# Up projection: six row tiles in halves, operands one tile ahead, another order of banks; final norm of the first half among the last products

## The chip, the cores and the metric

One core of one Trainium2 chip runs the whole program in one launch. The metric is the device time of one execution in microseconds (us); the median of three runs is quoted. TensorE (PE) multiplies, VectorE (DVE) and ScalarE (ACT) prepare operands and evacuate results, GpSimd (POOL) issues some DMAs, SyncE (SP) issues most of them.

## The reference, cut to what matters

A diffusion block over 512 latent tokens of width 2048: attention and a short convolution with adaLN modulation, an output projection with a gated residual, and then the part that is changed:

```
hf_l = modulate(rms_norm(x, g_ffn_norm), sh_f, sc_f)
u = dwconv3(hf_l @ w_up, cw, cb)          # 2048 -> 2 x 5504, width-3 convolution over tokens
a, g = jnp.split(u, 2, axis=-1)
x = x + gt_f * ((a * silu(g)) @ w_down)   # 5504 -> 2048
return rms_norm(x, g_final)
```

All of it is float32. Each float32 product is made of three products of rounded parts (high by high, high by low, low by high).

## The kernel before

**Layout.** Activations lie transposed: 16 tiles of 128 features by 512 tokens. An operand is a pair of tiles, `h` (rounded by ACT, a CAST) and `l` (the rest, a subtraction on DVE). `mm3` issues the three products; L168, L169 and L170 are its lines.

**First pairs of the up projection.** The 86 column tiles of `w_up` go in 43 pairs (gate and value). The first three pairs (`G` = 6 column tiles, tiles `uf`) are made row by row: for each of the 16 row tiles k, `first_weights(k)` loads and splits 6 weight tiles (`ufr`, `ufw`), `hf_tile(k)` normalises and modulates x (times `rl` on DVE at L854, scale and shift on ACT at L855, CAST at L857, subtraction at L858), and `row` issues 18 products. The first `EARLY` = 4 row tiles are made in token halves `H0` and `H1`, since the norm of `H0` is known before that of `H1`; their weights are held for both. `t_sums(j)` forms sums of halves (`T`, and new values in the second halves of `hf`) for the other 40 pairs, which a scheme with seven smaller products per pair makes (`product`, tiles `u3` to `u42`).

**Norms.** `rms_steps` is a generator: products with ones over the squares (L281), square root on ACT (L259), reciprocal on DVE (L260), a product that spreads the result over partitions (L265), a copy to `rl` (L288). `pump` takes it a step further between other work.

**Banks.** PSUM has eight banks. As built, `uf` has banks 7, 4, 5, 6 (pair 0's gate and value, pair 1's) and 2 and 3 (pair 2's). `bank8` then hands out banks in turn, three per pair (a, b, c), so u3 has banks 0, 1 and 2. `acts` frees the banks of `uf` pair by pair (convolution at L921 to L923, Silu at L929).

**The end.** The last group of the down projection has four output tiles (12 to 15); its last 8 of 43 row tiles are made for `H0`, then for `H1`. Per output tile and half that is 24 products, `down_end` (residual, DVE at L1127) and the square (ACT). The final norm of `H0` runs amid the products of `H1`; `final` multiplies by it (DVE at L1134) and stores two tiles at a time, eight stores of 256 KB per half, all from SP (L1135).

**What sets the order.** The program is written in the order of the source, but a scheduler of the tile framework orders each engine's instructions when it builds. Engines then run their own lists in order and wait for one another by semaphores.

Of the kernel before, what the change touches and what calls it, by code (L numbers as in the profile page):

```python
# [10 lines left out]
F32 = mybir.dt.float32  # L11
F32R = mybir.dt.float32r
AF = mybir.ActivationFunctionType
ALU = mybir.AluOpType
# [3 lines left out]
P = 128  # L18
# [3 lines left out]
NK = D // P  # L22
# [8 lines left out]
ORDER = [*range(7, 25), *range(7), *range(25, 31)]  # L31
G = 6

EARLY = 4

BANKS = [0, 1, 7, 4, 5, 6, 2, 3]
CTX_EARLY = 6
# [3 lines left out]
LAST = 8  # L41

AHEAD = 3


_SM = {}
# [12 lines left out]
def block_kernel(ctx, tc, xt, ctxt, ctxn, c, c_ctx, w_ada, small, w_in, w_inc, w_q, w_kv, w_out,  # L59
# [115 lines left out]
    def pump(n=1):  # L175
        while n and bg:
            if next(bg[0], bg) is bg:
                bg.popleft()
            else:
                n -= 1  # L180

    def drain():
        pump(-1)
# [14 lines left out]
    rl = con.tile([P, T], F32, name="rl")  # L198
# [617 lines left out]
    def row(pss, w, x, k, cols=slice(0, T)):  # L816

        for g in range(G):
            mm3(pss[g][:, cols], w[g], tuple(z[:, cols] for z in x), k == 0 and cols.start == 0, k == NK - 1)
# [25 lines left out]

    hf = {}

    def hf_tile(j, cols=slice(0, T)):
        if j not in hf:
            hf[j] = tuple(t2([P, T], F32R, f"hf{j}{z}") for z in "hl")  # L850
        sc = tiny(1, f"fs{j}")
        scale_of(sc, s("g_ffn", j), mod[:, 64 + j:65 + j])
        xr = xres[j][:, cols]
        V.tensor_tensor(out=xr, in0=xr, in1=rl[:, cols], op=ALU.mult)  # L854
        A.activation(xr, xr, AF.Identity, bias=mod[:, 48 + j:49 + j], scale=sc)  # L855
        hi, lo = (z[:, cols] for z in hf[j])
        A.copy(out=hi, in_=xr)  # L857
        V.tensor_tensor(out=lo, in0=xr, in1=hi.bitcast(F32), op=ALU.subtract)  # L858

    def hf_early():  # L860
        for j in range(3):
# [64 lines left out]
    def acts(f, g, a):  # L926

        ug = conv3(NF + f, g, f"g{f}")
        A.activation(ug, ug, AF.Silu)  # L929
        ua = conv3(f, a, f"a{f}")  # L930
        V.tensor_tensor(out=ua, in0=ua, in1=ug, op=ALU.mult)  # L931
        G_.dma_start(y_d[f], ua)  # L932
# [11 lines left out]
    def t_sums(j):  # L944

        e, o = xres[2 * j], xres[2 * j + 1]
        i, c = j // 2, HS[j % 2]
        if j % 2 == 0:
            for n in (1, 2, 4):
                TT[n, i] = tuple(t2([P, T], F32R, f"T{n}{i}{z}") for z in "hl")  # L950

        def put(dst, src):
            hi, lo = dst
            A.copy(out=hi, in_=src)
            V.tensor_tensor(out=lo, in0=src, in1=hi.bitcast(F32), op=ALU.subtract)

        V.tensor_tensor(out=e[:, H0], in0=e[:, H0], in1=e[:, H1], op=ALU.subtract)
        V.tensor_tensor(out=e[:, H1], in0=o[:, H1], in1=e[:, H1], op=ALU.subtract)
        put(half_of(hf[2 * j], 1), e[:, H1])
        V.scalar_tensor_tensor(out=o[:, H1], in0=e[:, H0], scalar=-1.0, in1=o[:, H1], op0=ALU.mult, op1=ALU.subtract)  # L960
        V.scalar_tensor_tensor(out=o[:, H0], in0=o[:, H1], scalar=-1.0, in1=o[:, H0], op0=ALU.mult, op1=ALU.subtract)
        for n, src in ((1, e[:, H0]), (2, o[:, H1]), (4, o[:, H0])):
            put(tuple(z[:, c] for z in TT[n, i]), src)
# [8 lines left out]
    def first_weights(k, held=False):  # L972

        raw = raw4(f"ufr{k}")
        SP.dma_start(raw[:, :G * P], w_up_first[k // 2][:, k % 2 * G * P:(k % 2 + 1) * G * P])
        if held:
            w = [hilo(raw[:, a:a + n], n, f"ufw{k}_{a}") for a, n in ((0, 4 * P), (4 * P, 2 * P))]
            return [part(w[g // 4], g % 4) for g in range(G)]
        w = split4(raw[:, :G * P], G * P, f"ufw{k}")
        return [part(w, g) for g in range(G)]  # L980
# [10 lines left out]
        return r  # L991

    pss = first_banks("uf")
    held = {}
    for h in range(2):
        for k in range(EARLY):
            if h == 0:
                held[k] = first_weights(k, k == EARLY - 1)
            if h or k > 2:
                hf_tile(k, HS[h])  # L1000
            row(pss, held[k], hf[k], k, HS[h])
            pump(1)
            if h and k % 2:
                t_sums(k // 2)
        drain()
    for k in range(EARLY, NK):
        if k == NK - 4:
            raws = up_load(G // 2)
        w = first_weights(k)
        hf_tile(k)  # L1010
        row(pss, w, hf[k], k)
        if k % 2:
            t_sums(k // 2)

    ph_ps.close()
    p8 = ctx.enter_context(tc.tile_pool(name="p8", bufs=1, space=PSUM, reuse_waits="tile"))
    banks = deque(BANKS)

    def bank8(nm):
        banks.rotate(-1)  # L1020
        return p8.tile([P, 512], F32, tag=f"s{banks[-1]}", bufs=1, name=nm)

    one_bank[0] = bank8

# [39 lines left out]
    for f in range(G // 2, NF):  # L1064
        a11, a12, s1, s3, a22 = raws
        if f + 1 < NF:
            raws = up_load(f + 1)
        else:
            down_ahead()
        pa, pb, pc = (bank8(f"u{f}{z}") for z in "abc")  # L1070
        cg = cp.tile([P, T], F32, tag="cg", bufs=2, name=f"cg{f}")
        ca = cp.tile([P, T], F32, tag="ca", bufs=2, name=f"ca{f}")
        product(pa, a11, "11", f"u{f}p1", True)
        u1 = aside(pa, f"u{f}1")
        product(pb, a12, "21", f"u{f}p2", True)
        V.tensor_tensor(out=cg[:, H0], in0=pb[:, :256], in1=u1, op=ALU.add)
        V.tensor_tensor(out=a11, in0=a11, in1=s1, op=ALU.add)  # L1077
        V.tensor_tensor(out=a12, in0=a12, in1=a11, op=ALU.add)  # L1078
        if pend is not None:
            finish(pend)  # L1080
        else:
            acts(*first_acts[0])
        product(pa, a11, "2", f"u{f}p6", False)
        u2 = aside(pa, f"u{f}2")
        product(pc, s1, "1", f"u{f}q5", True)
        if pend is None:
            for z in first_acts[1:]:
                acts(*z)
        product(pa, s3, "3", f"u{f}p7", False)
        u3 = aside(pa, f"u{f}3")  # L1090
        V.scalar_tensor_tensor(out=ca[:, H1], in0=pc[:, :256], scalar=-1.0, in1=u3, op0=ALU.mult, op1=ALU.subtract)
        pend = f, a22, a12, u2, u3, pa, pc, cg, ca
    finish(pend)

# [34 lines left out]
    def final(h, r, scaled):  # L1129

        rr = r.unsqueeze(1).to_broadcast([P, 2, T // 2])
        for j in range(0, NK, 2):
            o = scaled[j] if j in scaled else scale_out(j, h)
            ins = V.tensor_tensor(out=o, in0=o, in1=rr, op=ALU.mult)  # L1134
            SP.dma_start(out[j:j + 2, :, HS[h]].rearrange("a p t -> p a t"), o)  # L1135
            yield ins

    def scale_out(j, h):
# [9 lines left out]
    for g, (m0, n) in enumerate(DG):  # L1148
        ps = [bank8(f"d{g}{i}") for i in range(n)]
        tail = LAST if g == len(DG) - 1 else 0  # L1150
        for k in range(NF - tail):
            w, y = down_operands()
            for i in range(n):
                mm3(ps[i], part(w, i), y, k == 0, k == NF - 1 - tail)
            if g == 0 and k % 2:
                late_both(ada_late)
            if k == NF // 2:
                x_load(range(m0, m0 + n))
            if todo and k > 2:
                m = todo.pop(0)  # L1160
                if m:
                    add_squares(ssq, xl[m], T, f"eq{m}")
                else:
                    A.activation(ssq, xl[0], AF.Square)
        if not tail:
            for i in range(n):
                down_end(m0 + i, ps[i])
            todo = list(range(m0, m0 + n))
            continue
        last = [down_operands(held=True) for _ in range(tail)]  # L1170
        outs = []
        for h in range(2):
            sqs = [ssq]
            for i in range(n):
                for q, (w, y) in enumerate(last):
                    mm3(ps[i][:, HS[h]], part(w, i), half_of(y, h), False, h == 1 and q == tail - 1, on_top=True)
                end = down_end(m0 + i, ps[i], HS[h])
                x = xl[m0 + i][:, HS[h]]
                if i < n - 2:
                    add_squares(ssq, x, T // 2, f"eq{m0 + i}{h}", a=h * T // 2)  # L1180
                else:
                    sqs.append(add_squares(None, x, T // 2, f"eq{m0 + i}{h}", a=h * T // 2))
                pump(1)
            if h == 0:
                bg.append(rms_steps(sqs, D, 0, T // 2, rl, wait=1, one=True))
                outs = final(0, rl[:, HS[0]], {j: scale_out(j, 0) for j in range(0, m0, 2)})
            else:
                scaled = {j: scale_out(j, 1) for j in range(0, m0, 2)}
    drain()
    with tc.issue_after(end.ins):  # L1190
        next(outs)
    *_, r = rms_steps(sqs, D, T // 2, T // 2, None, one=True)
    for ins in outs:
        keep(ins)
# [101 lines left out]
```

## Time and profile before

| | |
|---|---|
| median of 3 runs | 2233.03 us (2226.94 to 2234.53) |
| the profiled execution | 2233.31 us, span 2231.5 us |
| TensorE busy | 2160.8 us, 97% of the span |
| VectorE busy | 1599.9 us, 72% |
| ScalarE busy | 1009.9 us, 45% |
| granted TensorE clock, mean | 0.990 of full |

The span is the time from the first to the last instruction in the trace; 1.8 us of the profiled execution lie outside it.

### The profile page before, as it was taken

The page shows a single profiled execution, that of the slowest core. Times are in us where ns is not written, and L with a number is a line of the kernel's source. Part 1 is how long each engine was busy: PE and PEld are TensorE (multiplying, and loading weights), DVE is VectorE, ACT ScalarE, POOL GpSimd, SP SyncE. Part 2 cuts the span into 40 slices and gives each one's busy share as a digit, 9 for nine tenths or more (in the row PEclk, how much of TensorE's full clock was granted, in tenths as well). Part 3 has the DMA queues.
Part 4 walks back from the last instruction along what each step waited for, and adds up shares of the span by engine and source line. Part 5 has one row for each costly group of instructions (what it writes and reads, how often), then busy time and mean ns, then how long its engine had stood idle before and what let it go on. Part 6 is the DMA issues. An engine that isn't in the chain of part 4 may idle for free.

```text
span 2231.5 us, 34462 instructions
## 1 busy us (share of the span) xinstructions
PE 2160.8 (97%) x13310; PEld 1927.4 (86%) x13310; DVE 1599.9 (72%) x2485; ACT 1009.9 (45%) x1629; POOL 111.1 (5%) x149
## 2 busy tenths in 40 slices
PE   7999999999999998999999999999999999999997
PEld 4788888878888887899999999999999888888886
DVE  7998887678796848677777777777777773633543
ACT  5533333554442246455545555555555432532443
POOL 0000000000000000011110111011110000000000
PEclk9999999999999999999999999999999999999998
DMA  8989883434469824477777777777776995752562
GB/s 330 345 279 332 276 282 120 142 123 156 161 243 359 317 98 125 120 197 203 190 192 199 203 193 191 199 197 202 188 198 196 346 348 166 238 172 90 174 199 76
DMA packets 144264, 466.75 MB, mean 209 GB/s; under 512 B 16290, under 2 KB 20642, under 8 KB 138082
## 3 DMA queue, kind: packets, MB, share of 16 engines
q1 hardware_dynamic: 127828, 407.13, 54.0%
q0 software_dynamic: 16272, 57.42, 12.6%
q8 instruction: 104, 1.70, 0.3%
q14 instruction: 60, 0.49, 0.1%
HBM read 442.73 MB, written 20.71 MB: 208 GB/s over the span
## 4 chain that ended last, share of the span: by engine, by line
PE 89%; DVE 5%; DMA 2%; ACT 2%; issue 1%; SPq 0%; POOL 0%; DVEq 0%; ACTq 0%
PE d L168 7%; PE d L169 7%; PE d L170 7%; PE pp L168 3%; PE pp L170 3%; PE pp L169 3%; PE o L170 1%; PE o L169 1%; PE o L168 1%; PE pf L169 1%; PE pf L170 1%; PE of L170 1%; PE pf L168 1%; PE of L168 1%; PE of L169 1%
## 5 line engine op out<-in xcount | busy, mean ns | idle before, releaser
L990 POOL DMA_DIRECT2D u_s<-in_w_up x80 | 68.0, 849 | 433.6 <-DMA u_s<-in_w_up 317.9
L151 ACT CAST w_0h<-rw 128x512 fp32r<-128x512 f32 (+1 forms) x63 | 38.3, 618 | 108.1 <-PE pp L169 65.3
L214 DVE SCALAR_TENSOR_TENSOR ada<-ada,sv 128x1024 f32<-128x1024 f32 x64 | 77.8, 1224 | 3.3 <-DMA ada<-in_w_ada 3.0
L489 DVE SCALAR_TENSOR_TENSOR ada<-ada,svc 128x1024 f32<-128x1024 f32 x64 | 76.1, 1223 | 1.2 <-DMA ada<-in_w_ada 1.1
L236 DVE SCALAR_TENSOR_TENSOR ra<-ra,sv 128x1024 f32<-128x1024 f32 x50 | 59.5, 1220 | 0.0
L152 DVE TENSOR_TENSOR w_0l<-rw,w_0h 128x512 fp32r<-128x512 f32 (+1 forms) x63 | 42.9, 686 | 22.2 <-ACT w_0h L151 22.2
L236 DVE SCALAR_TENSOR_TENSOR ada<-ada,sv 128x1024 f32<-128x1024 f32 x46 | 55.8, 1222 | 1.8 <-DMA ada<-in_w_ada 1.8
L1078 DVE TENSOR_TENSOR u<-u,u 128x1024 f32<-128x1024 f32 x40 | 49.0, 1225 | 1.3
L1077 DVE TENSOR_TENSOR u<-u,u_s 128x1024 f32<-128x1024 f32 x40 | 48.8, 1221 | 0.0
L932 POOL DMA_DIRECT2D y_d<-a x43 | 24.7, 574 | 389.9 <-DVE a L931 380.1
L730 POOL TENSOR_TENSOR gr<-gr,half 128x8 f32<-128x8 f32 x4 | 8.3, 2083 | 644.2 <-DVE mx L682 506.2
L236 DVE SCALAR_TENSOR_TENSOR adl<-adl,sv 128x1024 f32<-128x1024 f32 x32 | 38.9, 1220 | 0.1
L681 DVE TENSOR_REDUCE mx<-s 128x1 f32<-128x768 f32 x32 | 30.5, 955 | 10.2 <-PE s L671 10.2
L702 DVE TENSOR_TENSOR ptl<-t,pth 128x384 fp32r<-128x384 f32 x64 | 33.3, 551 | 4.2 <-ACT pth L701 4.2
L500 DVE TENSOR_TENSOR acc<-acc,pp 128x512 f32<-128x512 f32 x50 | 34.4, 688 | 2.2 <-PE pp L170 2.1
L701 ACT CAST pth<-t 128x384 fp32r<-128x384 f32 x64 | 28.5, 487 | 15.8 <-PE t L698 15.6
L921 ACT ACTIVATE g<-cg,sm 128x512 f32<-128x512 f32 x40 | 32.6, 814 | 0.0
L685 ACT ACTIVATE p<-s,mx 128x768 f32<-128x768 f32 x32 | 29.3, 916 | 6.5 <-DVE mx L682 6.5
L929 ACT ACTIVATE g<-g 128x512 f32<-128x512 f32 x43 | 27.2, 634 | 11.0 <-DVE g L923 10.9
L921 ACT ACTIVATE a<-ca,sm 128x512 f32<-128x512 f32 x40 | 32.0, 801 | 0.0
L1127 DVE SCALAR_TENSOR_TENSOR xl<-d,mod,xl 128x512 f32<-128x512 f32 (+1 forms) x20 | 12.4, 640 | 26.5 <-PE d L170 26.5
L698 PE MATMUL t<-io,p 128*128 128x128 f32 x192 | 27.5, 274 | 3.8 <-ACT p L685 2.5
(15572 smaller groups left out, 8766.4 us busy)
## 6 DMA issues: line engine op xcount, KB each, us to landing
ada<-in_w_ada SPq DMA_DIRECT2D x174, 512.0 KB, 5.9
u<-in_w_up SPq DMA_DIRECT2D x120, 512.0 KB, 8.0
u_s<-in_w_up SPq DMA_DIRECT2D x80, 512.0 KB, 4.1
u_s<-in_w_up POOLq DMA_DIRECT2D x80, 512.0 KB, 9.2
d<-in_w_dn SPq DMA_DIRECT2D x86, 384.0 KB, 3.7
y<-y_d SPq DMA_DIRECT2D x129, 256.0 KB, 4.9
ra<-in_w_ada SPq DMA_DIRECT2D x25, 1024.0 KB, 4.7
adl<-in_w_ada SPq DMA_DIRECT2D x32, 512.0 KB, 6.1
```

Source lines behind the costliest of these rows:

```text
L151: A.copy(out=hi[:, :n], in_=raw[:, a:a + n])
L152: V.tensor_tensor(out=lo[:, :n], in0=raw[:, a:a + n], in1=hi[:, :n].bitcast(F32), op=ALU.subtract)
L168: PE.matmul(ps, w[0], x[0], start=first, stop=False, skip_group_check=on_top)
L169: PE.matmul(ps, w[0], x[1], start=False, stop=False, skip_group_check=on_top)
L170: PE.matmul(ps, w[1], x[0], start=False, stop=last, skip_group_check=on_top)
L214: V.scalar_tensor_tensor(out=r, in0=r, scalar=1.0, in1=vec[:, i * 1024:(i + 1) * 1024], op0=ALU.mult, op1=ALU.mult, accum_out=col[:, i:i + 1])
L236: keep(V.scalar_tensor_tensor(out=r, in0=r, scalar=1.0, in1=svs[i], op0=ALU.mult, op1=ALU.mult, accum_out=lc[:, t % 4:t % 4 + 1] if i else ...
L489: keep(V.scalar_tensor_tensor(out=raw[q], in0=raw[q], scalar=1.0, in1=svc[:, q * 1024:(q + 1) * 1024], op0=ALU.mult, op1=ALU.mult, accum_o ...
L921: A.activation(u, src, AF.Identity, bias=s("fb", m), scale=s("fw", 86 + m))
L990: G_.dma_start(r[-1], src[more], accum_op=ALU.add)
L1077: V.tensor_tensor(out=a11, in0=a11, in1=s1, op=ALU.add)
L1078: V.tensor_tensor(out=a12, in0=a12, in1=a11, op=ALU.add)
```

## The change

`EARLY` goes from 4 to 6, and all six tiles' weights are loaded and split ahead of the first `H0` row; tiles 3, 4 and 5 of `hf` follow at once for `H0`. From tile 6 on, `prepare(k + 1)` stands ahead of `row(k)`. In `hf_tile` the multiplication by `rl` must come after the subtraction of the tile but one before it (`issue_after`). Eight empty tiles fix which bank a name has, so `BANKS` now means real banks: u3 has 0, 1 and 7, u4 has 4, 5, 6, u5 has 2, 3, 0. At the end the steps of the first half's norm are pumped at `NORM_AT` inside the products of `H1`, seven of its eight results are made among the last two output tiles' work, and every second store goes out from ACT.

```diff
-EARLY = 4
+EARLY = 6
+NORM_AT = [(0, 3), (0, 7), (1, 7)]
...
+    hf_last = [None, None]
     def hf_tile(j, cols=slice(0, T)):
...
-        V.tensor_tensor(out=xr, in0=xr, in1=rl[:, cols], op=ALU.mult)
+        with tc.issue_after(hf_last[0]) if hf_last[0] is not None else ExitStack():
+            V.tensor_tensor(out=xr, in0=xr, in1=rl[:, cols], op=ALU.mult)
...
-        V.tensor_tensor(out=lo, in0=xr, in1=hi.bitcast(F32), op=ALU.subtract)
+        ins = V.tensor_tensor(out=lo, in0=xr, in1=hi.bitcast(F32), op=ALU.subtract)
+        hf_last[:] = hf_last[1], ins.ins
...
-    held = {}
-    for h in range(2):
-        for k in range(EARLY):
-            if h == 0:
-                held[k] = first_weights(k, k == EARLY - 1)
-            if h or k > 2:
-                hf_tile(k, HS[h])
-            row(pss, held[k], hf[k], k, HS[h])
-            pump(1)
-            if h and k % 2:
-                t_sums(k // 2)
-        drain()
-    for k in range(EARLY, NK):
-        if k == NK - 4:
-            raws = up_load(G // 2)
+    held = [first_weights(k, k > 2) for k in range(EARLY)]
+    for k in range(3, EARLY):
+        hf_tile(k, H0)
+    for k in range(EARLY):
+        row(pss, held[k], hf[k], k, H0)
+        pump(1)
+    drain()
+    for k in range(EARLY):
+        hf_tile(k, H1)
+        row(pss, held[k], hf[k], k, H1)
+        pump(1)
+        if k in (3, 5):
+            t_sums(k // 2 - 1)
+    drain()
+    def prepare(k):
         w = first_weights(k)
         hf_tile(k)
+        return w
+    nxt = prepare(EARLY)
+    sums = deque(range(EARLY // 2 - 1, EARLY // 2))
+    for k in range(EARLY, NK):
+        w = nxt
+        if k + 1 < NK:
+            if k == NK - 4:
+                raws = up_load(G // 2)
+            if k == NK - 2:
+                t_sums(sums.popleft())
+            nxt = prepare(k + 1)
         row(pss, w, hf[k], k)
         if k % 2:
-            t_sums(k // 2)
+            sums.append(k // 2)
+            t_sums(sums.popleft())
+    for j in sums:
+        t_sums(j)
...
+    def bank_of(i, nm):
+        return p8.tile([P, 512], F32, tag=f"s{i}", bufs=1, name=nm)
     def bank8(nm):
         banks.rotate(-1)
-        return p8.tile([P, 512], F32, tag=f"s{banks[-1]}", bufs=1, name=nm)
+        return bank_of(banks[-1], nm)
+    for i in range(8):
+        bank_of(i, f"bank{i}")
...
-        else:
-            acts(*first_acts[0])
+        while first_acts:
+            acts(*first_acts.pop(0))
...
-            SP.dma_start(out[j:j + 2, :, HS[h]].rearrange("a p t -> p a t"), o)
+            (A if j % 4 else SP).dma_start(out[j:j + 2, :, HS[h]].rearrange("a p t -> p a t"), o)
...
                 for q, (w, y) in enumerate(last):
                     mm3(ps[i][:, HS[h]], part(w, i), half_of(y, h), False, h == 1 and q == tail - 1, on_top=True)
-                end = down_end(m0 + i, ps[i], HS[h])
+                    if (i, q) in NORM_AT:
+                        pump(1)
+                if h and i > 1:
+                    for _ in range(4 if i == 2 else 3):
+                        next(outs)
+                down_end(m0 + i, ps[i], HS[h])
...
-                pump(1)
...
-    drain()
-    with tc.issue_after(end.ins):
-        next(outs)
     *_, r = rms_steps(sqs, D, T // 2, T // 2, None, one=True)
     for ins in outs:
         keep(ins)
```

Three places in the built program matter. The first is DVE's list from the second half of the norm (`x` are the input tiles, `hf0l` the low part of operand tile 0; 128x256 is half a tile). Before, from the subtraction of tile 3:

```order
L858 TENSOR_TENSOR hf3l<-x_6559,hf3h 128x256
L854 TENSOR_TENSOR x_6539<-x_6539,rl 128x256
L854 TENSOR_TENSOR x_6545<-x_6545,rl 128x256
L854 TENSOR_TENSOR x_6552<-x_6552,rl 128x256
L854 TENSOR_TENSOR x_6559<-x_6559,rl 128x256
L854 TENSOR_TENSOR x_6566<-x_6566,rl 128x512
...
L854 TENSOR_TENSOR x_7251<-x_7251,rl 128x512
L957 TENSOR_TENSOR x_6539<-x_6539 128x256
L858 TENSOR_TENSOR hf0l<-x_6539,hf0h 128x256
```

Now, at the same place:

```order
L860 TENSOR_TENSOR x_6539<-x_6539,rl 128x256
L860 TENSOR_TENSOR x_6545<-x_6545,rl 128x256
L964 TENSOR_TENSOR x_6539<-x_6539 128x256
L257 SCALAR_TENSOR_TENSOR fs_7995<-mod,sm 128x1
L257 SCALAR_TENSOR_TENSOR fs_8045<-mod,sm 128x1
L864 TENSOR_TENSOR hf0l<-x_6539,hf0h 128x256
L860 TENSOR_TENSOR x_6552<-x_6552,rl 128x256
L864 TENSOR_TENSOR hf1l<-x_6545,hf1h 128x256
```

Before, sixteen multiplications stand ahead of the first low part; now two, and from there a multiplication and a subtraction take turns.

The second is ACT's list where u3 begins (`u3q5h` is the high part of the weights of the first product into bank c). Now:

```order
L921 CAST u3p6h<-u_11_8195 128x1024
L928 ACTIVATE g_8475<-uf_7577,sm 128x512
L936 ACT_TABLE_LOAD
L936 ACTIVATE g_8453<-g_8453 128x512
L936 ACTIVATE g_8464<-g_8464 128x512
L936 ACTIVATE g_8475<-g_8475 128x512
L928 ACTIVATE a_8480<-uf_7577,sm 128x512
L921 CAST u3q5h<-u_s_8199 128x1024
```

Nothing moved here: these operations stand in this order before too, and DVE's list from there on is also the same; only the banks behind the names `u3c`, `u4a` and so on are others.

The third is DVE's list at the end (`xl` are output tiles, `out` results, times `rl` for the first half, times `rs` for the second). Before:

```order
L1127 SCALAR_TENSOR_TENSOR xl_21091<-d_20539,mod,xl_21091 128x256
L1127 SCALAR_TENSOR_TENSOR xl_21093<-d_20540,mod,xl_21093 128x256
L1134 TENSOR_TENSOR out_21601<-out_21601,rl 128x512
L260 RECIPROCAL rr<-rr 128x2
L1134 TENSOR_TENSOR out_21604<-out_21604,rl 128x512
```

Now:

```order
L1163 TENSOR_TENSOR out_21677<-out_21677,rl 128x512
L318 TENSOR_TENSOR eq<-eq,eq_21749 128x256
L1163 TENSOR_TENSOR out_21680<-out_21680,rl 128x512
L1163 TENSOR_TENSOR out_21815<-out_21815,rl 128x512
L1156 SCALAR_TENSOR_TENSOR xl_21155<-d_20603,mod,xl_21155 128x256
L1156 SCALAR_TENSOR_TENSOR xl_21157<-d_20604,mod,xl_21157 128x256
L262 RECIPROCAL rr<-rr 128x2
L1163 TENSOR_TENSOR out_21853<-out_21853,rl 128x512
L1163 TENSOR_TENSOR out_21823<-out_21823,rs 128x512
```

Before, one of the eight results of the first half stands ahead of the last reciprocal; now seven do, ahead of the residuals of the last two output tiles, and one follows it. In ACT's list the stores of the second, fourth and sixth result now stand ahead of the squares of the last two tiles.

## Rows read from the trace of the kernel before

**Rows 1.** Who waited for whom, TensorE, whole span: total, times, longest us.
```profile
PE uf L169 <- DVE hf0l L858: 6.6, 1, 6.6
PE u3c L168 <- DVE a L923: 5.2, 1, 5.2
```

**Rows 2.** Timeline of TensorE, first pairs: start us, us, what, xcount [idle before].
```profile
841.94 0.28 PE L168 MATMUL uf<-hf3h,ufw_0h 128*128 128x256 f32 x1
...
844.09 0.60 PE L265 MATMUL rs<-io,rr 128*128 128x128 f32 x4
847.04 0.86 PE L168 MATMUL uf<-hf0h,ufw0h 128*128 128x256 f32 x5 [2.34 <-ACT hf0h L857]
854.52 0.58 PE L169 MATMUL uf<-hf0l,ufw0h 128*128 128x256 f32 x1 [6.62 <-DVE hf0l L858]
...
865.51 1.44 PE L168 MATMUL uf<-hf4h,ufw4h 128*128 128x512 f32 x5 [1.14 <-ACT hf4h L857]
...
916.17 0.28 PE L168 MATMUL u3a<-hf0h,u3p1h 128*128 128x256 f32 x1
```

**Rows 3.** Timeline of ScalarE, VectorE and SyncE's queue, same place.
```profile
831.78 0.33 SPq L975 DMA_DIRECT2D ufr<-in_w_up_first  x1
836.92 0.61 ACT L298 CAST ufw_0h<-ufr 128x512 fp32r<-128x512 f32 x1
837.73 0.40 ACT L857 CAST hf3h<-x 128x256 fp32r<-128x256 f32 x1
845.14 8.66 DVE L854 TENSOR_TENSOR x<-x,rl 128x256 f32<-128x256 f32 x16 [6.21 <-ACT rl L288]
846.60 0.39 ACT L857 CAST hf0h<-x 128x256 fp32r<-128x256 f32 x1
854.04 0.43 DVE L858 TENSOR_TENSOR hf0l<-x,hf0h 128x256 fp32r<-128x256 f32 x1
```

**Rows 4.** DMA issues of that stretch: KB each, median us to landing.
```profile
ufr<-in_w_up_first SPq DMA_DIRECT2D x12, 384.0 KB, 5.5
```

**Rows 5.** Windows: length, busy PE, PEld, DVE, ACT, POOL, clock, DMA share, GB/s.
```profile
845.00:907.00 62.00, 52.12 (x249) 43.62 (x250) 50.26 (x113) 37.73 (x75) 2.62 (x3) 0.92 0.39 104
928.00:930.00 2.00, 2.00 (x11) 2.00 (x11) 2.00 (x3) 0.00 (x0) 0.54 (x1) 0.50 0.40 139
```

**Rows 6.** Timeline where u3 begins, TensorE, VectorE and ScalarE.
```profile
925.38 1.03 ACT L914 CAST u3q5h<-u_s 128x1024 fp32r<-128x1024 f32 x1
926.30 0.75 DVE L923 SCALAR_TENSOR_TENSOR a<-uf,sm,a 128x511 f32<-128x511 f32 x1
927.20 0.55 PE L168 MATMUL u3c<-T10h,u3q5h 128*128 128x256 f32 x1 [5.17 <-DVE a L923]
933.09 0.37 PE L168 MATMUL u3c<-T10h,u3q5h 128*128 128x256 f32 x1
```

**Rows 7.** Timeline of the end, all engines and SyncE's queue.
```profile
2204.20 0.28 PE L168 MATMUL d<-yh235h,dw235h 128*128 128x256 f32 x1
2207.08 0.50 PE L281 MATMUL rs<-io,eq 128*128 128x1 f32 x4
2212.06 0.38 ACT L288 COPY rl<-rs 128x256 f32<-128x256 f32 x1 [1.80 <-PE rs L265]
2215.40 0.42 ACT L312 ACTIVATE eq151t<-xl 128x256 f32<-128x256 f32 x1 [2.25 <-DVE xl L1127]
2216.88 4.28 DVE L1134 TENSOR_TENSOR out<-out,rl 128x512 f32<-128x512 f32 x7
2217.02 1.23 PE L265 MATMUL rs<-io,rr 128*128 128x128 f32 x4 [0.55 <-DVE rr L260]
2221.08 4.87 DVE L1134 TENSOR_TENSOR out<-out,rs 128x512 f32<-128x512 f32 x8
```

**Rows 8.** Windows at the end, columns as in rows 5.
```profile
2208.00:2217.00 9.00, 8.17 (x69) 8.00 (x68) 2.36 (x7) 4.39 (x10) 0.00 (x0) 0.98 0.01 5
2219.00:2230.00 11.00, 0.00 (x0) 0.00 (x0) 6.95 (x12) 0.00 (x0) 0.00 (x0) 0.50 1.00 341
```

More of the change, by code (lines that the diff above doesn't have):

```diff
@@ L1085, in block_kernel @@
         product(pc, s1, "1", f"u{f}q5", True)
-        if pend is None:
-            for z in first_acts[1:]:
-                acts(*z)
         product(pa, s3, "3", f"u{f}p7", False)
@@ L1091, in block_kernel @@
         V.scalar_tensor_tensor(out=ca[:, H1], in0=pc[:, :256], scalar=-1.0, in1=u3, op0=ALU.mult, op1=ALU.subtract)
+        if first_acts:
+            acts(*first_acts.pop(0))
         pend = f, a22, a12, u2, u3, pa, pc, cg, ca
```

## The prediction

> **What bounds the kernel now.** TensorE is busy for 97% of the span, so I read first the view of who waited for whom, for TensorE alone [rows 1]: of its waits the two longest, 6.6 and 5.2 us, lie where the change does its work. Then I read the timeline around each, to see which list is late, and last the end, where TensorE is done and DVE and the stores set the time.
>
> In the first pairs [rows 2] the reader is to see an `H0` row of 18 products take 2.15 us (841.94 to 844.09), and then nothing at full pace: five products after 2.34 us of waiting, the rest after 6.62 more. DVE's rows say why [rows 3]: `rl` of the second half is there at 845.14, but DVE multiplies sixteen tiles by it (8.66 us) before it makes the low part of tile 0 (854.04), though its high part was ready at 846.99 (846.60 + 0.39). TensorE waits for an order, not for work.
>
> At u3 [rows 6] the first product into bank c starts at 927.20, after the last convolution of pair 2 (926.30 + 0.75), which frees bank 2. But that product also needs `u3q5h`, whose CAST ends at 926.41 (925.38 + 1.03). The two conditions are 0.6 us apart.
>
> At the end [rows 7, 8] DVE makes seven results of the first half from 2216.88 and the eight of the second from 2221.08, and the stores keep the DMA engines at a share of 1.00 (341 GB/s) from 2219 to 2230, though they were idle from 2208 to 2217 (0.01).
>
> **The change, part by part.** *First pairs.* Before, 841.94 to 916.17 took 74.2 us. In it 12 full rows took 50.66 us (865.51 to 916.17), 4.22 each. Now from 841.94 come the spread product (0.6), three more `H0` rows, six `H1` rows (nine at 2.15) and ten full rows (42.2): 62.2 us. The gain is 12.1 us if TensorE doesn't wait. What has to hide, in order:
> - *Two more weight tiles are split before operand 3.* A pair of CASTs takes 0.81 us (836.92 to 837.73), so `hf3h` moves from 837.73 to about 839.4 and the operands 3 to 5 are complete near 842.6 (three more operations of 0.4 to 0.6 us each, taking turns). Their rows start at 842.5, 844.7 and 846.8: hidden. Of the loads, the sixth is issued at 831.78 and lands about 5.5 us later [rows 4], 837.3, before its CAST near 838.5.
> - *`rl` for the second half.* The spread product moves from 844.09 to 841.94; DVE can use `rl` 1.05 us later (844.09 to 845.14), at 843.0. The first half tile is complete 1.85 us on (845.14 to 846.99) plus 0.43 for the low part, at 845.3; its row starts at 849.0. The stall of rows 1 goes, with 3.7 us to spare.
> - *DVE's whole load.* What lies between 845 and 907 is 50.3 us of DVE work [rows 5]. Now it starts at 843.0 and must be done, but for a few sums, when row 15 starts, at 849.0 + 12.9 + 9 x 4.22 = 899.9: 56.9 us for 50.3. The 1.1 us wait for `hf4h` [rows 2] is an order of the same kind and goes too. DVE may wait 6.6 us in all; before, it waited 11.7 in that stretch, mostly for the sixteen multiplications' aftermath and for weight buffers that TensorE still read. Each weight buffer comes free two full rows (8.4 us) ahead of its use and its split takes under 1 us, so I take no loss; the bounds are 0 and 5.1 us (the old waits, all of them).
>
> *Banks.* u3's bank c is now that of pair 0's gate, freed some 8 us earlier. What is late next is `u3q5h`: ACT's and DVE's lists up to it are unchanged, so it still ends 14 us into the same chain. The stall shrinks from 5.17 to about 4.4 us: 0.7 us gained, not 5.2. That all three `acts` calls now stand together in the source moves nothing in those lists. After the stall the granted clock stood at 0.50, the lower level of 1.2 GHz, with 11 products in 2 us [rows 5] against 17 in a row at full pace (2.0 x 18 / 2.15), until 933.09: 5.9 us, of which 2.1 are lost by the products (6 of 17) and 2.95 by the clock; I take 2.6. A stall of 4.4 us is nearer to 5.17 than to none, so I take the same loss again; bounds 0 and 2.6 us gained.
>
> The Trainium skill, "TensorE: Matmul & The Clock Gate", section "Why this matters for your kernels", says that a long enough idle gap between bursts sends the array back to half rate. The trace agrees (0.50 after 5.17 us); by it the loss stays.
>
> *The end.* The sums of the first half stood after two output tiles of `H1` (2207.08); now they stand after one, 2.88 us earlier (2204.20), and the spread moves with them, so `rl` comes at 2212.44 - 2.9 = 2209.5. DVE then has seven results at 0.60 (4.28 for seven, overlapping) and one square-sum: to 2214.2. That is 2.4 us late for output tile 14's residual, but tile 15's comes at 2214.8 as before, and with it the last square at 2215.40, the last reciprocal and the spread product that ends at 2218.25. Of the stores, ACT issues three ahead of those squares. They wait for DVE's sixth result, near 2213.5; no store from ACT is in this trace. An issue's cost lies between nothing and the 0.77 us in which 256 KB move at 341 GB/s [rows 8], and even that ends by 2214.5, before the last square: 0. The seven stores drain between 2211 and 2217 through idle DMA engines.
>
> From 2218.25 DVE has only the second half's eight results: the first at 2218.95, the last at 2223.1 rather than 2225.95. Eight stores of 256 KB at 341 GB/s take 0.77 us each, 6.15 us. In the old order data flowed from about 2218.6 and fifteen stores ended at 2230.1; now eight start about 1 us after 2218.95 and end at 2226.1, 4.0 us earlier. By the last result alone, 2223.1 for 2225.95, the gain is 2.9. The share of 1.00 says that the stores set the end, so I take 3.8, near the upper of the two.
>
> A rule that speaks against this edit: the Trainium skill, "DMA: Bandwidth & Descriptors", section "Issuing engines are not separate DMA queues": stores from several engines share the same DMA engines, so spreading them saves only issue time. The share of 1.00 agrees, and by it the second queue gains nothing. My 3.8 rests on the earlier seven stores alone.
>
> **Sum.** 12.1 + 0.7 + 3.8 = 16.6 us from the profiled execution's 2233.31, which is 0.3 us from the median: 2216.7 us.
>
> **The rivals.**
> - *The banks free u3 altogether* (its stall and the slow products go: 5.2 + 2.6 in place of 0.7). For: the trace names only the bank as the releaser. Against: the CAST at 926.41 and unchanged lists. 2233.3 - 12.1 - 7.8 - 3.8 = 2209.6.
> - *DVE or ACT becomes the bound of rows 6 to 15.* For: 50.3 us of DVE work in 56.9. Against: the buffers' lead of two rows. With the 5.1 us lost: 2221.8.
> - *The end gives nothing*, because ACT's stores hold back the last square, or the stores are slower from two queues: 2220.5. Against: over 1 us of slack per store.
> - *Slower than before: DVE's fixed order.* Each split of weights now waits, with the next operands queued behind it on DVE, for TensorE to leave the row three before. If that makes every one of the ten full rows take 1.7 us longer (5.9 us for 4.22), 17 us are gone and the change loses; at 2.2 us each it ends near 2238.7. Against: DVE has about 4 us of work per row, and its list has operands ahead of the splits.
> - *The change doesn't do what it says.* For the banks nearly so; that is in the sum.
>
> **How the numbers follow.** The forecast has 0.70, the u3 rival 0.08, DVE as bound 0.13, no gain at the end 0.06, DVE's order with a loss 0.03. The range takes in the second and third, and the unknown costs above (up to 2.6 us gained at u3, 0.9 lost at the end) with some 3 us for the spread of runs: 2210 to 2223. About 0.3% (6.7 us) is what a measurement of this kernel can tell from no change. All cases but the last lie over 9 us below 2233: faster 0.93, within 0.3% 0.05, slower 0.02.
>
> **What would show it.** Right: no TensorE wait over 1 us between the first `uf` product and u3; u3's first product about 62 us after the first product of row 3; one wait of 4 to 5 us at u3c, now for ACT's `u3q5h`, and products at half rate behind it; seven results before 2215 in the old time frame, and stores that end about 4 us earlier after the last square. Wrong: waits for `hf` or `ufw` in rows 6 to 15, DVE busy without a gap there, no stall at u3c, or a last square that is late behind ACT's stores.

## The result, and the profile after

The changed kernel takes 2210.03 us in the median of 11 runs (2206.8 to 2220.03); the kernel before, run beside it, 2226.87 us (11 runs, 2223.61 to 2234.53). The ratio is 0.9924, 95% interval 0.9907 to 0.9941: 16.8 us less, where 16.6 were forecast. The time itself lies 6.7 us under the forecast of 2216.7, at the lower edge of the range (2210). So the size of the change came out near the forecast, and the time that it was taken from did not: 2233 us isn't where the kernel before usually runs (over all 55 of its runs on record the median is 2228.2, and 20 lie above 2231). That 16.8 meets 16.6 so closely is in part luck: the interval leaves room from 13.1 to 20.7 us, and in the traces the three terms come to some 18.0 (12.6, 0.85 and 4.5).

TensorE's waits in the changed kernel, as total, times and longest (the others of over 2 us lie outside the change and stood before too):

```profile
PE u3c L170 <- ACT u3q5h L921: 4.3, 1, 4.3
PE uf L170 <- ACT ufw0h L921: 1.7, 1, 1.7
```

Of the two waits of [rows 1] the first is gone; the second is shorter and has another releaser, the cast that the prediction named. The 1.7 us for `ufw0h`, at the very first product of the first pairs, stood in the trace before too.

The timeline of TensorE, from the spread product to u3 (start, length, what, idle before):

```profile
840.25 0.61 PE L267 MATMUL rs<-io,rr 128*128 128x128 f32 x4
840.62 0.72 PE L170 MATMUL uf<-hf3h,ufw_0h 128*128 128x256 f32 x4
...
847.17 0.28 PE L170 MATMUL uf<-hf0h,ufw0h 128*128 128x256 f32 x1
847.29 0.27 PE L171 MATMUL uf<-hf0l,ufw0h 128*128 128x256 f32 x1
...
901.87 0.29 PE L170 MATMUL u3a<-hf0h,u3p1h 128*128 128x256 f32 x1
...
912.13 0.58 PE L170 MATMUL u3c<-T10h,u3q5h 128*128 128x256 f32 x1 [4.32 <-ACT u3q5h L921]
```

Against [rows 2]: from the spread product to u3's first product 61.62 us now, without a wait; the stretch that stands for it before, from 841.94 to 916.17, had 74.2. The second half's rows start at 847.17, right behind the sixth `H0` row.

VectorE and ScalarE at the same places:

```profile
841.30 0.76 DVE L860 TENSOR_TENSOR x<-x,rl 128x256 f32<-128x256 f32 x2 [1.77 <-ACT rl L290]
843.18 0.43 DVE L864 TENSOR_TENSOR hf0l<-x,hf0h 128x256 fp32r<-128x256 f32 x1
843.52 0.42 DVE L860 TENSOR_TENSOR x<-x,rl 128x256 f32<-128x256 f32 x1
...
910.38 0.76 ACT L928 ACTIVATE a<-uf,sm 128x512 f32<-128x512 f32 x1
911.04 1.03 ACT L921 CAST u3q5h<-u_s 128x1024 fp32r<-128x1024 f32 x1
```

Where [rows 3] had sixteen multiplications in a row, there are now two, and the low part of tile 0 is complete 3.6 us before its row starts (843.61, 847.17). At u3 the cast stands where it stood, behind everything that it stood behind.

Windows, with columns as in [rows 5] (length, busy PE, PEld, DVE, ACT, POOL, clock, DMA share, GB/s):

```profile
834.50:837.50 3.00, 3.00 (x17) 3.00 (x17) 3.00 (x8) 2.46 (x7) 0.00 (x0) 0.57 1.00 391
840.25:901.87 61.62, 61.62 (x348) 53.72 (x347) 53.00 (x119) 41.27 (x81) 3.46 (x4) 1.00 0.51 125
912.50:915.50 3.00, 3.00 (x16) 3.00 (x16) 2.97 (x5) 0.80 (x1) 0.54 (x1) 0.50 0.22 86
```

TensorE is busy for all of the first pairs from row 3 on, at the full clock, and VectorE for 53.0 of 61.6 us. Behind the wait at u3c the clock is again at its lower level, 1.2 GHz; so it is, without forecast, for some 3 us soon after the first products.

The end, all engines, and the queue of ScalarE's stores (`ACTq`):

```profile
2187.50 3.10 DVE L1163 TENSOR_TENSOR out<-out,rl 128x512 f32<-128x512 f32 x5 [0.48 <-ACT rl L290]
2188.82 3.12 ACTq L1164 DMA_DIRECT2D out<-out  x3
2192.05 0.47 DVE L1156 SCALAR_TENSOR_TENSOR xl<-d,mod,xl 128x256 f32<-128x256 f32 x1
2192.41 0.28 PE L172 MATMUL d<-yh242h,dw242l 128*128 128x256 f32 x1
2193.34 0.40 ACT L314 ACTIVATE eq151t<-xl 128x256 f32<-128x256 f32 x1
2194.95 0.71 PE L267 MATMUL rs<-io,rr 128*128 128x128 f32 x4 [0.55 <-DVE rr L262]
2195.70 4.87 DVE L1163 TENSOR_TENSOR out<-out,rs 128x512 f32<-128x512 f32 x8 [0.22 <-PE rs L267]
```

From the end of the last down product (2192.69) to the end of the span (2204.9) are 12.2 us; before, 2214.78 to 2231.5 were 16.7. The residual of tile 14 is late behind the seven results (2192.05), and the last square is not: it starts 0.93 us after the last product did, 0.90 before (2214.50, and 2215.40 in [rows 7]).

### The profile page after: what moved, and what is told of

The parts are those of the page before. It is cut to its first block, busy times and chain, and to the rows that moved or that the text cites. A ratio compares the mean times of both kernels' runs of the same rounds, so it can differ in the third digit from the quotient of the medians.

```text
span 2204.9 us, 34542 instructions
## 1 busy us (share of the span) xinstructions
PE 2149.2 (97%) x13346; PEld 1914.2 (87%) x13346; DVE 1599.0 (73%) x2493; ACT 1010.5 (46%) x1635; POOL 111.3 (5%) x149
## 4 chain that ended last, share of the span: by engine, by line
PE 91%; DVE 4%; DMA 2%; ACT 2%; issue 1%; SPq 0%; POOL 0%; DVEq 0%; ACTq 0%
PE d L170 7%; PE d L172 7%; PE d L171 7%; PE pp L170 4%; PE pp L172 4%; PE pp L171 4%; PE o L172 1%; PE o L171 1%; PE o L170 1%; PE uf L170 1%; PE uf L171 1%; PE uf L172 1%; PE of L172 1%; PE pf L171 1%; PE of L170 1%; PE of L171 1%
## 5 line engine op out<-in xcount | busy, mean ns | idle before, releaser
L936 ACT ACTIVATE g<-g 128x512 f32<-128x512 f32 x43 | 27.2, 633 | 12.1 <-DVE g L930 12.1
L929 DVE SCALAR_TENSOR_TENSOR g<-cg,sm,g 128x511 f32<-128x511 f32 x40 | 29.8, 745 | 0.0
```

## The experiments

All of these compute the whole reference. Times are medians. A ratio is to the kernel before, run beside the kernel in question; it need not be the quotient of the medians. In the three sets of runs that follow, the kernel before has medians of 2226.86 us (24 runs; before_again, bank_only, uf_only, end_only), 2229.98 (11; before_third, u3_first, all_sp, no_hold) and 2229.87 (9; u3_first2, early4, late_norm, no_ahead), so medians of different sets are not to be compared to better than some 3 us. For the parts I take, from each trace, the starts of five products: the first of the first pairs, the first of product p6 of u3, of u5 and of u41, and the last high-by-high product of row tile 35 in the down projection; and the end of the span. "Per pair" is u5 to u41 over 36.

| kernel | first pairs to u3 | u3 to u5 | per pair | u41 to down 35 | to the end |
|---|---|---|---|---|---|
| before | 92.8 | 42.5 | 20.16 | 515.3 | 20.2 |
| before_again | 92.8 | 41.1 | 20.16 | 515.6 | 20.2 |
| before_third | 94.3 | 40.8 | 19.94 | 517.5 | 20.3 |
| bank_only | 93.6 | 40.8 | 19.94 | 517.7 | 20.2 |
| uf_only | 80.1 | 41.8 | 19.94 | 517.7 | 20.2 |
| end_only | 94.4 | 40.9 | 19.94 | 515.6 | 15.8 |
| after | 80.9 | 40.9 | 19.94 | 518.3 | 15.3 |
| no_hold | 82.0 | 40.8 | 19.94 | 518.5 | 15.7 |
| early4 | 82.8 | 41.2 | 20.16 | 517.9 | 15.3 |
| no_ahead | 79.4 | 41.1 | 20.16 | 518.8 | 15.3 |
| all_sp | 81.0 | 41.9 | 19.94 | 517.7 | 15.3 |
| late_norm | 81.0 | 42.0 | 19.94 | 517.9 | 18.0 |
| u3_first | 78.9 | 41.3 | 20.16 | 517.6 | 15.3 |
| u3_first2 | 76.1 | 41.4 | 19.94 | 518.5 | 15.8 |

Four things in it come and go with the execution. The first column is about 1.5 us longer where the clock fell to 1.2 GHz soon after the first products (in before_third, bank_only, end_only, after, all_sp, late_norm and u3_first2). The second is about 1 us longer where the lower clock behind the wait at u3c lasted 6.9 us and not 3.4 (in before, uf_only, all_sp and late_norm). A pair takes 19.94 or 20.16 us. And the fourth column has 515.3 to 515.6 us in before, before_again and end_only and 517.5 or more in the others, before_third among them.

**Which 2233?** The kernel before, unchanged, for two more traces.

> The kernel before, once more, for a second trace of it. In the two traces at hand the pairs u5 to u41 of the up projection, which the change doesn't touch but for the numbers of their banks, take 20.16 us each before and 19.94 after, 8 us over 36 pairs. Theory A (the pace differs from run to run or chip to chip): here a pair may take 19.9 to 20.0 us and the time is 2224 to 2229. Theory B (the banks or places of the kernel before set the pace): a pair takes 20.16 us again.

> The kernel before, a third trace. A pair u5 to u41 took 20.16 us in both traces of it (times 2233.3 and 2232.3) and 19.94 in all four of other kernels, two of which have the same banks. Theory A (two paces that come and go with the execution): if the time is under 2229, a pair takes 19.94 us here too. Theory B (the build of the kernel before has the slower pace): 20.16 whatever the time.

Measured: 2232.32 us with 20.16 a pair (by itself theory B's result), and 2228.85 us with 19.94, both on chip 1 by the record. One window over 360 us of the pairs, of before, of before_third and of after, in that order, each from its own trace:

```profile
1300.00:1660.00 360.00, 360.00 (x3002) 360.00 (x3001) 269.10 (x305) 187.38 (x250) 40.91 (x54) 1.00 0.74 195
```

```profile
1300.00:1660.00 360.00, 360.00 (x3036) 360.00 (x3036) 273.08 (x308) 189.71 (x254) 41.12 (x55) 1.00 0.73 199
```

```profile
1300.00:1660.00 360.00, 360.00 (x3036) 360.00 (x3035) 272.92 (x308) 189.01 (x252) 41.40 (x55) 1.00 0.74 199
```

TensorE is busy throughout and the granted clock is 1.00 in all three, yet 3002 products fit in one and 3036 in the others. The same kernel does both on one chip, so it is neither the build nor the chip, and of before_third's theories A stands: 8.1 us over 36 pairs (0.224 each) that come and go. What sets the pace no run here shows.

**The parts alone.** The bank numbers alone (kernel before, with the eight empty tiles):

```diff
+    def bank_of(i, nm):
+        return p8.tile([P, 512], F32, tag=f"s{i}", bufs=1, name=nm)
     def bank8(nm):
         banks.rotate(-1)
-        return p8.tile([P, 512], F32, tag=f"s{banks[-1]}", bufs=1, name=nm)
+        return bank_of(banks[-1], nm)
+    for i in range(8):
+        bank_of(i, f"bank{i}")
```

> The kernel before with the bank numbers alone fixed. Theory A (the wait at u3c is ScalarE's cast of u3q5h): the wait of 5.17 us becomes about 4.4, the time falls by 0.7 us, at most 3.3 if the clock then falls for a shorter stretch: ratio 0.9985 to 1. Theory B (banks set the pace of the pairs): a pair of u5 to u41 takes 19.94 us and the time falls by 8 us more, ratio 0.996.

Measured: 2227.36 us (12 runs), ratio 0.999 (0.9973 to 1.0007), and this wait:

```profile
PE u3c L168 <- ACT u3q5h L914: 4.4, 1, 4.4
```

5.2 us have become 4.4, with the cast as releaser, and the time doesn't move by what can be measured: theory A. Its pairs take 19.94 us, but so they do with the old banks (uf_only, end_only), so theory B falls.

The first pairs alone (`EARLY`, the weights ahead, `prepare`, `issue_after`, all as in the change's diff):

> The kernel before with the first pairs of the change alone. Theory A (my sum): no wait over 1 us between the first uf product and u3, some 62 us from row 3's first product to u3's, 12 us less than before; ratio 0.9945. Rival (the rest of the gain comes of banks and end): 8 us or less. The wait at u3c stays 5.2 us on DVE's convolution.

Measured: 2213.99 us (5 runs), ratio 0.9927 (0.9902 to 0.9952). The first column falls by 12.7 us from either of the two traces of before that had no lower clock at its start, and TensorE has no wait in the first pairs but the 1.7 us at their start: theory A. The wait at u3c stays:

```profile
PE u3c L168 <- DVE a L928: 5.1, 1, 5.1
```

The end alone (`NORM_AT`, seven results early, every second store from ScalarE):

> The kernel before with the end of the change alone. Theory A: from the last down product to the end 16.7 us become 12.2 (the trace after has 12.2), the time falls by 3.8 to 4.5 us, ratio 0.998. Rival (the end is faster only since the clock stood higher there after): under 2 us.

Measured: 2224.03 us (10 runs), ratio 0.9977 (0.996 to 0.9995). From the end of the last down product (2205.95) to the end of the span (2218.7) it has 12.75 us, 4.0 less than before. The other half us of the changed kernel lies in the clock, not in the order. Its spread product, to set beside the one of after (0.71):

```profile
2208.21 1.22 PE L267 MATMUL rs<-io,rr 128*128 128x128 f32 x4 [0.55 <-DVE rr L262]
```

So the rival falls: the order alone is worth 4 us.

**What in the first pairs does it?** Without the rule for VectorE's order:

```diff
-        with tc.issue_after(hf_last[0]) if hf_last[0] is not None else ExitStack():
-            V.tensor_tensor(out=xr, in0=xr, in1=rl[:, cols], op=ALU.mult)
+        V.tensor_tensor(out=xr, in0=xr, in1=rl[:, cols], op=ALU.mult)
```

> The changed kernel without the rule that holds a multiplication by rl behind the subtraction of the tile but one before. Theory A (VectorE's sixteen multiplications ahead of the first low part made the long wait before): the multiplications stand in front again and a wait for hf0l of about 2 us (6.6 before, less the 3.7 to 5 us that six half rows give) comes back; 2 to 6 us slower than the changed kernel, with the clock. Rival (six half rows alone cover it): no wait over 1 us in the first pairs, the same time.

Measured: 2210.69 us (4 runs), ratio 0.9908 (0.9878 to 0.9937). TensorE's wait, then VectorE's row for it:

```profile
PE uf L171 <- DVE hf0l L863: 2.3, 1, 2.3
```

```profile
845.84 6.77 DVE L859 TENSOR_TENSOR x<-x,rl 128x256 f32<-128x256 f32 x12
```

The multiplications stand in front again and the wait is back, at 2.3 us; the first column is 82.0, 2.6 us over no_ahead (below), whose start had the same clock. The wait is of theory A's size; in whole times this kernel can't be told from the changed one.

Four early tiles in place of six (`EARLY = 4`, all else as in the change):

> The changed kernel with EARLY at 4 and all else as it is. Theory A: the half rows left are the cover of rl for the second half: four H0 rows of 2.15 us in place of six, so 4.3 us less cover, and the low part of tile 0 was 3.7 us early by my sum: a wait of 0.5 to 2 us for hf0h or hf0l at the second half. Rival (EARLY is the larger part of the gain): waits of 4 us or more, 5 us slower than the changed kernel.

Measured: 2216.78 us (4 runs), ratio 0.9939 (0.9917 to 0.9962).

```profile
PE uf L170 <- ACT hf0h L863: 2.3, 1, 2.3
PE uf L171 <- DVE hf4l L864: 0.8, 1, 0.8
```

3.1 us of waits, 3.4 us in the first column (82.8 against 79.4 in no_ahead, whose start had the same clock): more than theory A's wait, less than the rival's. The 2.34 us for `hf0h` of [rows 2] are back with VectorE's new order in place, so they are what the norm takes from the last `H0` row; six `H0` rows cover them, four don't.

The operands prepared right before their row:

```diff
-    nxt = prepare(EARLY)
...
-        w = nxt
...
-            nxt = prepare(k + 1)
+        w = prepare(k)
         row(pss, w, hf[k], k)
```

> The changed kernel with weights and operand of a row prepared in the source right before it, not a row ahead; the scheduler still orders each engine, and TensorE's list stays nearly the same. Theory A (from tile 6 on the engines have slack, the source's place matters little): no wait over 1 us in rows 6 to 15, time within 0.1% of the changed kernel. Rival (VectorE or ScalarE would bound these rows without the row of lead): waits for hf or ufw of 2 us or more.

Measured: 2214.03 us (6 runs), ratio 0.9915 (0.989 to 0.994); no wait in the first pairs but the 1.7 us at their start, first column 79.4. Theory A for the waits; its 0.1% in time is finer than the interval. The lists did not come out alike: from the operand of tile 8 on VectorE and ScalarE have another order than in the changed kernel, and still TensorE doesn't wait. The tile of lead in the source buys nothing that shows here.

**What at the end does it?** All stores from SP, and the norm's steps where they were before:

```diff
-            (A if j % 4 else SP).dma_start(out[j:j + 2, :, HS[h]].rearrange("a p t -> p a t"), o)
+            SP.dma_start(out[j:j + 2, :, HS[h]].rearrange("a p t -> p a t"), o)
```

```diff
-NORM_AT = [(0, 3), (0, 7), (1, 7)]
+NORM_AT = [(0, 7), (1, 7), (2, 7)]
```

> The changed kernel with all stores from SP. Theory A (the earlier results alone gain at the end, the DMA engines are full): from the last down product to the end 12.2 us as in the changed kernel, within 0.4 us. Rival (the second queue gains by issuing faster): 1 us or more longer.

> The changed kernel with the steps of the first half's norm one output tile later, where they were before, and the seven results still ahead of the last residuals. Theory A (the 2.88 us by which the norm is earlier carry the gain at the end): rl comes 2.9 us later, VectorE's results then stand in front of the residual of tile 15, and the last square and the end come 1 to 3 us later than in the changed kernel. Rival (only the place of the results matters): the same end, 12.2 us after the last product.

Measured, all_sp: 2208.72 us (4 runs), ratio 0.9895 (0.9861 to 0.9929), 15.3 us in the last column, as in after. The second queue gains nothing: theory A. By the Trainium skill, "DMA: Bandwidth & Descriptors", section "Issuing engines are not separate DMA queues", it can save only the time of issuing; this run agrees, and shows no gain from that either.

Measured, late_norm: 2212.2 us (4 runs), ratio 0.9918 (0.9898 to 0.9937), 18.0 us in the last column; from the end of the last down product (2197.19) to the end of the span (2211.7) 14.5 us, 2.3 over after. VectorE's rows, then TensorE's wait:

```profile
2194.88 4.30 DVE L1163 TENSOR_TENSOR out<-out,rl 128x512 f32<-128x512 f32 x7 [0.48 <-ACT rl L290]
2199.10 0.48 DVE L1156 SCALAR_TENSOR_TENSOR xl<-d,mod,xl 128x256 f32<-128x256 f32 x1
```

```profile
PE rs L283 <- ACT eq151t L314: 2.2, 1, 2.2
```

The seven results push the residual of tile 15 behind them, the last square starts 2.76 us after the last product did (2199.67), 1.8 later than in after, and half of the gain is gone: theory A. So the earlier norm is worth about half (2.3 us), and the early results alone the other half, though they hold up the last residual. The earlier norm with the results at their old place was not run.

**The wait that is left.** ScalarE's list at u3 in another order: `u3q5h` and the copy of u3a stand ahead of the Silu of pairs 1 and 2.

```diff
...
+            for m, g, a in first_acts:
+                us.append((m, conv3(NF + m, g, f"g{m}"), conv3(m, a, f"a{m}", m == 2)))
+            gate(*us[0])
+            w6 = split4(a11, 1024, f"u{f}p6")
+            w5 = split4(s1, 1024, f"u{f}q5")
+            with tc.issue_after(behind[0]), tc.issue_after(behind[-1]):
+                gate(*us[1])
+                gate(*us[2])
...
```

(`conv3` is the three taps alone, `gate` the Silu, the product and the store; `behind` holds the copy and the casts.)

> The changed kernel with ScalarE's list at u3 in another order: the cast of u3q5h and the copy of u3a stand ahead of the Silu of pairs 1 and 2, and pair 2's value has a buffer of its own, so that it needn't wait for pair 0's. Theory A (ScalarE's late cast and copy are the cause of the wait at u3c): the wait of 4.3 us goes, and so do the products at the lower clock behind it (3.4 us, 1.7 lost): 6 us less than the changed kernel, ratio 0.990 to before. Rival (VectorE's convolutions are the cause, the cast only comes last): a wait of 2 us or more stays, for u3q5l or a VectorE tile, and under 3 us are gained.

Measured: 2208.69 us (6 runs), ratio 0.9905 (0.9878 to 0.9932); the wait is 3.7 us. Neither forecast came: the wait stays, as the rival had it, but still for the cast and not for VectorE. The cast is late for a new reason (VectorE's row, then ScalarE's):

```profile
914.10 0.74 DVE L931 SCALAR_TENSOR_TENSOR g<-uf,sm,g 128x511 f32<-128x511 f32 x1
```

```profile
914.88 0.78 ACT L929 ACTIVATE a<-uf,sm 128x512 f32<-128x512 f32 x1 [4.23 <-DVE g L931]
915.55 1.03 ACT L921 CAST u3q5h<-u_s 128x1024 fp32r<-128x1024 f32 x1
```

ScalarE's reading of pair 2's value waits for VectorE's last reading of its gate, which lies in the same tile of two banks. So in the second try both of ScalarE's readings come first:

```diff
-                us.append((m, conv3(NF + m, g, f"g{m}"), conv3(m, a, f"a{m}", m == 2)))
+                both = [conv_mid(NF + m, g, f"g{m}"), conv_mid(m, a, f"a{m}", m == 2)]
+                us.append((m, *(conv_sides(*c) for c in both)))
```

> As u3_first, with both of ScalarE's readings of pair 2 ahead of VectorE's: in u3_first the value's reading waited until VectorE had read the gate, in the same tile of two banks, and the cast behind it came 3.7 us late. Theory A (ScalarE's order, with that wait in it, makes the wait at u3c): the cast ends near 5.5 us after u3's first product, when TensorE needs it, the wait is under 0.5 us, no products at the lower clock follow; from the first uf product to u3a's product p6 75 us for 80.9 in the changed kernel, ratio 0.990 to before or better. Rival (VectorE is as late): a wait of 1 to 4 us for u3q5l or a VectorE tile takes its place.

Measured: 2207.1 us (4 runs), ratio 0.9893 (0.9871 to 0.9915). TensorE's wait, VectorE's row behind it, and the window around it:

```profile
PE u3c L172 <- DVE u3q5l L922: 1.5, 1, 1.5
```

```profile
915.83 1.21 DVE L922 TENSOR_TENSOR u3q5l<-u_s,u3q5h 128x1024 fp32r<-128x1024 f32 x1
```

```profile
911.00:920.00 9.00, 7.54 (x63) 7.33 (x62) 8.96 (x14) 4.67 (x8) 1.69 (x3) 1.00 0.46 138
```

The cast no longer holds TensorE; VectorE does, for 1.5 us, busy for 8.96 of 9 us, and behind this wait the clock stays at 1.00. The first column is 76.1, where theory A had 75. From the first pairs' first product to u5 117.5 us where after has 121.8, with the same lower clock at the start: 4.3 us less. ScalarE's order was the cause, and VectorE is late next: both theories have a part. In whole times it is the fastest of the kernels here, but the intervals overlap (after: 0.9907 to 0.9941).

## Why the prediction was wrong, and what of it held

*The base: wrong.* The step that failed is "the profiled execution's 2233.31, which is 0.3 us from the median". That median was of three runs, two of them at 2233 and 2234.5; of eleven it is 2226.87. The profiled execution is one with 20.16 us a pair (8.1 us more over the 36 pairs than in before_third). From 2226.87 the same sum gives 2210.3, for 2210.03 measured. The third of the three runs, 2226.94, told that a lower level exists; I gave "some 3 us for the spread of runs", where the base alone was 6.2 off. Later sets of runs put the base at 2230, so it is itself known to some 3 us, and the agreement of 2210.3 with 2210.03 is closer than that. The traces of before and after themselves differ by 26.6 us in span, which is not what the change gives: 8.1 of it is that pace, 3.1 lie ahead of the first pairs, where before has the lower clock more often, and some 2 go the other way in the fourth column of the table.

*First pairs: right.* 12.1 forecast, 74.2 to 61.62 measured, 12.6. The wait went for both reasons that the prediction gave, and the runs split them: VectorE's order is worth about 2.6 us once there are six early tiles, six tiles for four about 3.4 with that order. "TensorE waits for an order, not for work" fits the 6.62 us alone; the 2.34 ahead of them were the norm's, as early4 shows. The rest is not theirs one by one: without either, there are the 9.0 us of waiting (2.34 + 6.62) that [rows 2] show, and a clock at its lower level through it (0.50 from 848 to 858 in that trace).

*DVE or ACT as the bound of rows 6 to 15: didn't come.* The window from row 3 to u3 shows 8.6 us of VectorE idle and no wait of TensorE; nor did VectorE's fixed order cost TensorE a wait.

*Banks and u3: right in place, cause and size of the wait.* 4.4 us forecast, 4.3 measured, on the cast that was named; banks alone give 0.8 us. After it 1.2 GHz, as the forecast took over from before, but for 3.4 us of products and not 5.9. That is not the shorter wait's doing: behind the same wait of 5.2 us before_again and before_third have some 3.4 us at the lower level too, and behind 4.3 us all_sp and late_norm have 6.9. The loss of 2.6 us was read off one execution; no run here shows what sets its length. The rival that the banks free u3 altogether is refuted by bank_only.

*The end: right in kind, 0.7 too small.* 3.8 forecast, 4.5 in the changed kernel, 4.0 in end_only; the difference is the spread product at the higher clock. The residual of tile 14 came 2.2 us late (2192.05, where 2189.85 is 2.88 before tile 15's at 2192.73; 2.4 forecast), at no cost. The rival of ScalarE's stores holding back the last square didn't come.

*The clock.* The Trainium skill, "TensorE: Matmul & The Clock Gate", section "Why this matters for your kernels", has the idle gap bring the half rate. The runs agree for waits of 3.7 us and more at u3c. They show no fall behind the 1.5 us of u3_first2 or the 2.3 us of no_hold and early4; yet in seven of the fourteen traces the clock fell soon after the first products of the first pairs, behind a wait of 1.7 us. No run here shows why there, and why only at times.

## What to carry to other kernels

Before a sum is set against a profiled execution, compare the pace of a long uniform stretch with the spread of the times: three runs with two levels in them are not a base, and a range has to reach from both. When a wait names its releaser, look at what else ends within a microsecond of it: freeing the bank moved 0.8 of 5.2 us, because a cast was next, and behind the cast a vector operation. Work that is moved into idle time on an engine with a fixed order pays in full only if its input is early too; moving the results without the norm gave up half of the gain.

## What was not expected of the hardware

The same products, with TensorE busy throughout and the granted clock at 1.00, run at two paces: 3002 or 3036 in 360 us, 20.16 or 19.94 us a pair, constant over the whole stage of one execution. Both occur with the same kernel on the same chip (before_again, before_third), and with variants of the changed one (u3_first 20.16, u3_first2 19.94). Why stays open.
